# A norm's factors as a row through DRAM, and queries and keys of the retention computed transposed

## The chip, the cores and the metric

The kernel runs on one core of one Trainium2 chip. The metric is the device time of one execution in microseconds (us); lower is better. TensorE (PE in the profile) multiplies, VectorE (DVE) and ScalarE (ACT) work on its results, GpSimd (POOL) does little here, and SyncE (SP) issues nearly all DMAs, in one queue in order.

## The reference: what is computed

A trunk of two layers on x of 256 positions and 1024 columns, batch 1. Each layer has a half-step SwiGLU feed-forward (FFN, inner width 2816), a mixer, and another half-step FFN; each of these stands between a pre-norm and a post-norm and is added to x:

```python
h = swiglu(rms_norm(x, g[0]), ...);  x = x + 0.5 * rms_norm(h, g[1])
m = mixer(rms_norm(x, g[2]), ...);   x = x + rms_norm(m, g[3])
h = swiglu(rms_norm(x, g[4]), ...);  x = x + 0.5 * rms_norm(h, g[5])
```

`rms_norm(x, g)` is x times the position's factor 1/sqrt(mean(x^2) + eps), times the gain g of the column. Layer 0's mixer is dilated sliding-window attention (three groups of heads, their outputs merged); layer 1's is retention: 4 heads, one projection into queries q and keys k (256 columns a head each), values v (512) and two gates g_f and g_b (512 each), a rotation of q and k by the position's angles, and

```python
y_f = chunk_retention(q, k, v, log_gamma[0])              # decayed scores, forward
y_b = flip(chunk_retention(flip(q), flip(k), flip(v), log_gamma[1]))
y = silu(g_f) * head_group_norm(y_f) + silu(g_b) * head_group_norm(y_b)
out = y @ w_out
```

The rotation mixes the two halves of a head's 256 columns: (t1 cos - t2 sin, t1 sin + t2 cos).

## The kernel before, in words

All is float32, with each product made of three faster ones: an operand is split into a high part (a rounded copy, `fp32r`) and a low part (the rest), and `mm3` (lines 190 to 194) or the loop of `unit_t` adds high x high, high x low and low x high in PSUM. x is split in transposed form: `pre_half` transposes x of one tile of 128 positions (PE), copies the high part (ACT) and subtracts the low part (DVE) into `xh`, `xl`.

**The norm's factors are applied late.** The pre-norm's gain goes into the weights as they are split; the factor of the position (`rstd`, a column with one number per partition and tile, made by `pre_stats` and `rsqrt` on DVE while the next stage's first matmuls run) is applied to the projection's result. Where positions lie on partitions, `rstd` is the scale of the instruction that reads the result. Where they lie along the free axis, a row of 256 factors on every partition is needed. `rows` (lines 389 to 399) makes it: DVE multiplies the identity with each column of factors (`dg`), PE multiplies a matrix of ones with these diagonals (`rw`), DVE copies the result (`rows`). It is called once in each FFN and twice in attention (for q with the factor -0.125 in it, and for k).

**The weights' stream** (`Stream`). Weights come in loads of 1 MB (`dma`, line 83, or two loads of half a megabyte where a group takes columns from two places, as the retention's q and k) into two buffers `raw`. Each load makes two pieces; `split` makes a piece's high part on ACT and low part on DVE (lines 115 to 125) into a ring of six slots `w`, or, for the later pieces of a stage's first unit, into spare buffers (`wx`). When PE has used a piece, `done` splits the next one, and when a load's second piece is split the next load is issued. Pieces marked `still` lie at an offset of 16 elements in their slot.

**Units.** A projection goes in units of up to 512 columns, four pieces each, accumulated in two of six PSUM banks (`acc`). There are two forms. `unit` (lines 331 to 337) keeps x stationary and streams 512 columns of weights: 48 matmuls, results with positions on partitions ("natural"). `unit_t` (lines 368 to 387) keeps weights stationary and streams the 256 positions: 96 matmuls, results with columns on partitions ("transposed"). The first unit of each stage (`first_unit`) is natural, one tile of positions after the other, since x's second tile is ready later. In each unit, after the second piece, `flush` runs what was put into the list `pend`, and after every piece `work` runs two entries of the list `bg`. These lists and the order of the code give priorities; a scheduler orders each engine's instructions from them, ahead of the run, and the order on each engine is then fixed. DVE's order in the last part of a stage is that of the code.

**FFN** (`ffn`, `ffn_t`). Unit 0 (gate) and unit 1 (up) are natural, units 2 to 10 transposed; their gate results are multiplied with the row (line 350) before ACT's Silu. `rows` is put into `pend`, so that it runs in the middle of unit 1. Then comes `down`, the second projection.

**Attention** (`attn`). Units of q and k are transposed except the first; DVE multiplies them with the row while it stores them (line 662), q reversed within blocks of 64.

**Retention** (`plan_ret`, `ret`). For each head four natural units: q and k together ("qk"), v, g_f, g_b. At the start the rotation's tables (`rope`, positions on partitions) are scaled with `rstd` (line 872). After a qk unit DVE rotates each tile: two products with the tables (line 922), a difference and a sum (lines 925, 926) into `ro`. `rt_qk` (line 934) transposes the eight blocks of 128 x 128 on PE, and ACT copies them (line 935). `rt_scores` makes the scores of both chunks (line 944), multiplies them with the decay (line 946) and splits them; `rt_y` makes y forward (d = 0) or backward (d = 1); `rt_gate` normalises y and multiplies it with the Silu of the gate; `rt_store` transposes the sum and splits it for the output projection. In head 0 six empty entries stand ahead of the transposes and the scores in `bg`, so that they come at the end of the v unit and in the g_f unit; in heads 1 to 3 the transposes and the scores come after the second piece of the v unit.

The program's parts are, in this order: FFN, attention, FFN, FFN, retention, FFN. Every name of a tile in the profile leaves out numbers: `ac_f` are an FFN's accumulators, `at` attention's, `rt` the retention's, `d_f`, `d_at`, `d_rt` those of the second projections, `rqk` the transposed queries and keys, `rs` the scores, `rc` the tile that holds the copies of queries and keys and the decayed scores, `epsn` a reordered column of numbers that the second FFN moves by 4-byte DMAs, `gpost` the gain of a post-norm that is broadcast to all partitions.

## Time and profile before

| | |
|---|---|
| device time, median of 3 runs (lowest to highest) | 1292.06 us (1289.16 to 1293.95) |
| profiled execution: its device time | 1295.78 us |
| profiled execution: span from first to last instruction | 1294.0 us |
| mean granted TensorE clock | 0.998 |
| ScalarE and VectorE busy, of the span | 54% and 69% |
| first projection matmul of the retention to the last | 846.39 to 1054.1 us |

The device time of an execution is a little longer than the span of its instructions. Rows of a timeline give start, duration, engine, line, operation, tile written <- tiles read, shapes and the count of merged instructions; in brackets stands how long the engine idled before it and what ended that. Rows of the waits give who waited for whom, the total in us, the times, and the longest. Rows of one tile give minimum, median and maximum duration in ns. PE's matmuls are pipelined: a matmul's duration in a row is longer than the time from its start to the next one's start, so only the latter may be added up.

### The profile page before, as it was taken

The page shows a single profiled execution, that of the slowest core. Times are in us where ns is not written, and L with a number is a line of the kernel's source. Part 1 is how long each engine was busy: PE and PEld are TensorE (multiplying, and loading weights), DVE is VectorE, ACT ScalarE, POOL GpSimd, SP SyncE. Part 2 cuts the span into 40 slices and gives each one's busy share as a digit, 9 for nine tenths or more (in the row PEclk, how much of TensorE's full clock was granted, in tenths as well). Part 3 has the DMA queues.
Part 4 walks back from the last instruction along what each step waited for, and adds up shares of the span by engine and source line. Part 5 has one row for each costly group of instructions (what it writes and reads, how often), then busy time and mean ns, then how long its engine had stood idle before and what let it go on. Part 6 is the DMA issues. An engine that isn't in the chain of part 4 may idle for free.

```text
span 1294.0 us, 20715 instructions
## 1 busy us (share of the span) xinstructions
PE 1276.6 (99%) x8362; PEld 1136.7 (88%) x8362; DVE 889.4 (69%) x1593; ACT 695.5 (54%) x1073; POOL 19.7 (2%) x17
## 2 busy tenths in 40 slices
PE   8999999999999999999999999999999999999997
PEld 6999888987997879999889998877888888899986
DVE  6776557678567668866477665588887875767644
ACT  4655445467445557764456554455555545555442
POOL 1000001000000000000000000000000000000000
PEclk9999999999999999999999999999999999999999
DMA  7755566664764356665546565645564645565551
GB/s 217 229 186 193 189 217 192 200 200 146 201 198 153 130 162 221 196 196 179 192 163 209 187 195 194 197 147 175 155 184 144 186 165 195 168 200 176 190 195 65
DMA packets 130093, 235.72 MB, mean 182 GB/s; under 512 B 25404, under 2 KB 42284, under 8 KB 129997
## 3 DMA queue, kind: packets, MB, share of 16 engines
q1 hardware_dynamic: 129852, 234.14, 56.7%
q8 instruction: 65, 1.06, 0.3%
q14 instruction: 32, 0.25, 0.1%
q10 hardware_dynamic: 144, 0.26, 0.1%
HBM read 232.21 MB, written 1.12 MB: 180 GB/s over the span
## 4 chain that ended last, share of the span: by engine, by line
PE 90%; DVE 4%; ACT 2%; DMA 2%; issue 1%; SPq 0%; DVEq 0%; ACTq 0%
PE ac_f L381 10%; PE ac_f L382 10%; PE ac_f L383 10%; PE d_f L192 6%; PE d_f L193 6%; PE d_f L194 6%; PE rt L194 4%; PE rt L193 4%; PE rt L192 4%; PE at L382 3%; PE at L383 3%; PE at L381 3%; PE at L192 2%; PE at L194 2%; DMA raw<-in_ret_w_in_dram 2%; PE at L193 2%
## 5 line engine op out<-in xcount | busy, mean ns | idle before, releaser
L121 ACT ACTIVATE w<-raw,gcol 128x512 fp32r<-128x512 f32 x596 | 394.0, 715 | 309.0 <-PE ac_f L383 101.9
L122 DVE SCALAR_TENSOR_TENSOR w<-raw,gcol,w 128x512 fp32r<-128x512 f32 x596 | 418.1, 749 | 153.9 <-ACT w L121 150.6
L116 DVE TENSOR_TENSOR w<-raw,w 128x1024 fp32r<-128x1024 f32 x112 | 137.2, 1225 | 134.5 <-ACT w L115 134.2
L115 ACT ACTIVATE w<-raw 128x1024 fp32r<-128x1024 f32 x112 | 118.8, 1061 | 166.7 <-PE d_f L194 95.7
L192 PE MATMUL d_f<-w,hhf 128*128 128x512 f32 x352 | 137.2, 390 | 0.0
L193 PE MATMUL d_f<-w,hhf 128*128 128x512 f32 x352 | 137.0, 389 | 0.0
L194 PE MATMUL d_f<-w,hlf 128*128 128x512 f32 x352 | 137.0, 389 | 0.0
L382 PE MATMUL at<-xl_f,w 128*128 128x256 f32 x352 | 99.0, 281 | 0.0
L381 PE MATMUL at<-xh_f,w 128*128 128x256 f32 x352 | 99.0, 282 | 0.0
L383 PE MATMUL at<-xh_f,w 128*128 128x256 f32 x352 | 98.9, 281 | 0.0
L192 PE MATMUL rt<-w,xh_f 128*128 128x512 f32 x244 | 95.6, 392 | 0.2 <-ACT xh_f L238 0.2
L193 PE MATMUL rt<-w,xh_f 128*128 128x512 f32 x244 | 95.8, 392 | 0.0
L194 PE MATMUL rt<-w,xl_f 128*128 128x512 f32 x244 | 95.1, 390 | 0.0
L381 PE MATMUL ac_f<-xh_at,w 128*128 128x256 f32 x288 | 81.0, 281 | 0.0
L381 PE MATMUL ac_f<-xh_f,w 128*128 128x256 f32 x288 | 81.0, 281 | 0.0
L381 PE MATMUL ac_f<-xh_rt,w 128*128 128x256 f32 x288 | 81.0, 281 | 0.0
L383 PE MATMUL ac_f<-xh_f,w 128*128 128x256 f32 x288 | 80.9, 281 | 0.0
L383 PE MATMUL ac_f<-xh_rt,w 128*128 128x256 f32 x288 | 80.9, 281 | 0.0
L383 PE MATMUL ac_f<-xh_at,w 128*128 128x256 f32 x288 | 80.9, 281 | 0.0
L382 PE MATMUL ac_f<-xl_at,w 128*128 128x256 f32 x288 | 80.9, 281 | 0.0
L382 PE MATMUL ac_f<-xl_f,w 128*128 128x256 f32 x288 | 80.9, 281 | 0.0
L382 PE MATMUL ac_f<-xl_rt,w 128*128 128x256 f32 x288 | 80.9, 281 | 0.0
(346 smaller groups left out, 2835.8 us busy)
## 6 DMA issues: line engine op xcount, KB each, us to landing
raw<-in_ffn_w_down_dram SPq DMA_DIRECT2D x44, 1024.0 KB, 4.9
raw<-in_ffn_w_up_dram SPq DMA_DIRECT2D x40, 1024.0 KB, 5.0
raw<-in_ffn_w_gate_dram SPq DMA_DIRECT2D x39, 1024.0 KB, 5.0
raw<-in_attn_w_in_dram SPq DMA_DIRECT2D x36, 1024.0 KB, 5.1
raw<-in_ret_w_in_dram SPq DMA_DIRECT2D x24, 1024.0 KB, 5.6
raw<-in_ret_w_in_dram SPq DMA_DIRECT2D x16, 512.0 KB, 3.9
raw<-in_ret_w_out_dram SPq DMA_DIRECT2D x8, 1024.0 KB, 4.8
raw<-in_ffn_w_gate_dram SPq DMA_DIRECT2D x10, 512.0 KB, 4.0
```

Of the source, the lines that this page charges most:

```text
L115: nc.scalar.activation(hi, raw, AF.Copy)
L116: nc.vector.tensor_tensor(out=lo, in0=raw, in1=hi.bitcast(F32), op=ALU.subtract)
L121: nc.scalar.activation(hi[:, s], raw[:, s], AF.Copy, scale=gc)
L122: nc.vector.scalar_tensor_tensor(out=lo[:, s], in0=raw[:, s], scalar=gc, in1=hi[:, s].bitcast(F32), op0=ALU.mult, op1=ALU.subtract,)
L192: mm(out, xh, wh, start=start, stop=False)
L193: mm(out, xh, wl, start=False, stop=False)
L194: mm(out, xl, wh, start=False, stop=stop)
L381: mm(out, hi[:, s], xh, start=k == 0 and a == 0, stop=False, skip_group_check=True)
L382: mm(out, hi[:, s], xl, start=False, stop=False, skip_group_check=True)
L383: mm(out, lo[:, s], xh, start=False, stop=k == NK - 1, skip_group_check=True)
```

## The change

Three things, in one edit:

- `rows` and the matrix of ones go. `row_out` stores `rstd`, two numbers per partition, as 256 numbers in a row in DRAM (one DMA on SP), right behind the first unit of each FFN, of attention and of retention. `row_in` loads this row into every partition (one DMA on SP); it stands in `pend`, so in the middle of the second unit. FFNs take this row where they took `rows`; attention takes it for q and k, with the factor -0.125 now in the instruction, which for that becomes two half as wide.
- In retention the qk units are transposed ones (`unit_t`, pieces `still`), so that queries and keys come out of PSUM with the head's columns on partitions. The rotation's tables come transposed from the host's constants, cos and sin of all 256 positions beside each other; they are multiplied once with the row (in the second unit). The rotation makes, for q and for k, two products and a difference and a sum, and writes into the place from which the scores are made. The 32 transposes and 8 ACT copies of `rt_qk` go.
- In head 0 the units' order is g_f, qk, v, g_b instead of qk, v, g_f, g_b, so that the first unit remains natural. The Silu of g_f is made after the first unit; y forward, its gate and y backward are put into `bg` together, after the v unit. The six empty entries go.

The core of the diff:

```diff
-        self.ones = sb.tile([P, P], F32, name="ones")
-        nc.gpsimd.memset(self.ones, 1.0)
...
-            r = st["r"].unsqueeze(1).to_broadcast([P, 2, 2 * P])
+            r = self.row.unsqueeze(1).to_broadcast([P, 2, 2 * P])
...
-    def rows(self, cols, name):
...
+    def row_out(self, name):
+        self.factors = self.dram.tile([2 * P], F32, name=f"factors_{name}")
+        self.nc.sync.dma_start(self.factors[0 : 2 * P].rearrange("(t p) -> p t", p=P), self.rstd)
+
+    def row_in(self, name):
+        self.row = self.sb.tile([P, 2 * P], F32, tag="row", name=f"row_{name}")
+        self.nc.sync.dma_start(self.row, self.factors[0 : 2 * P].partition_broadcast(P))
...
                 self.first_unit(pieces, accs)
-                self.pend.append(lambda: st.update(r=self.rows(self.rstd, "f")))
+                self.row_out(name)
+                self.pend.append(lambda: self.row_in(name))
...
-                self.pend.append(lambda rq=rq: scales.update(q=self.rows(rq, "q"), k=self.rows(self.rstd, "k")))
+                self.row_out("at")
+                self.pend.append(lambda: self.row_in("at"))
...
-                        nc.vector.tensor_tensor(out=dst, in0=src, in1=sc.unsqueeze(1).to_broadcast([P, 2, 4, 64]), op=ALU.mult)
+                        for a in range(2):
+                            nc.vector.scalar_tensor_tensor(out=dst[:, a], in0=src[:, a], scalar=-0.125 if kind == "q" else 1.0, in1=sc, op0=ALU.mult, op1=ALU.mult)
...
-            units.append((h, "qk", self.ws.add_rows([w[:, q : q + 256], w[:, D + q : D + q + 256]], NK, n)))
...
+            for kind in ("qk", "v", "gf", "gb") if h else ("gf", "qk", "v", "gb"):
+                if kind == "qk":
+                    units.append((h, kind, self.ws.add_rows([w[:, q : q + 256], w[:, D + q : D + q + 256]], NK, n, True)))
...
                 self.first_unit(pieces, accs)
-                for t in range(2):
-                    nc.vector.tensor_scalar(out=self.rope[t], in0=self.rope[t], scalar1=self.rstd[:, t : t + 1], scalar2=None, op0=ALU.mult)
+                self.row_out("rt")
+                self.pend.append(lambda: self.row_in("rt"))
             else:
-                self.unit(pieces, accs)
+                (self.unit_t if kind == "qk" else self.unit)(pieces, accs)
             if kind == "qk":
+                if u == 1:
+                    nc.vector.tensor_tensor(out=self.rope, in0=self.rope, in1=self.row.unsqueeze(1).to_broadcast([P, 2, 2 * P]), op=ALU.mult)
...
-                if h:
-                    self.pend.append(lambda st=st: self.rt_qk(st))
-                    self.pend.append(lambda st=st: self.bg.append(lambda: self.rt_scores(st)))
-                else:
-                    skip = lambda: None
-                    self.bg += [skip] * 6 + [lambda st=st: self.rt_qk(st, (0,)), lambda st=st: self.rt_qk(st, (1,)), lambda st=st: self.rt_scores(st), skip]
+                for b in range(2):
+                    self.rotary(st, b, accs[b])
+                self.pend.append(lambda st=st: self.bg.append(lambda: self.rt_scores(st)))
...
                 self.bg.append(lambda st=st: self.rt_y(st, 0))
+                if h == 0:
+                    self.bg += [lambda st=st, sg=sg: self.rt_gate(st, 0, sg), lambda st=st: self.rt_y(st, 1)]
...
-                if d == 0:
+                if u == 0:
+                    pass
+                elif d == 0:
...
+        for i in range(2):
+            z = sb.tile([P, 512], F32, tag="pr", bufs=6, name=f"m{i}{st['h']}{b}")
+            m.append(z.rearrange("p (a c) -> p a c", a=2))
+            nc.vector.tensor_tensor(out=m[i], in0=a, in1=self.rope[:, ::-1] if i else self.rope, op=ALU.mult)
+        nc.vector.tensor_tensor(out=st["qk"][:, 2 * b, :], in0=m[0][:, 0], in1=m[0][:, 1], op=ALU.subtract)
+        nc.vector.tensor_tensor(out=st["qk"][:, 2 * b + 1, :], in0=m[1][:, 0], in1=m[1][:, 1], op=ALU.add)
```

More of the change, by code (lines that the diff above doesn't have):

```diff
@@ L387, in unit_t @@
             self.work(quota)
-    def rows(self, cols, name):
-        nc, sb = self.nc, self.sb
-        d = sb.tile([P, 2, P], F32, tag="dg", name=f"dg_{name}")
-        for t in range(2):
-            nc.vector.tensor_scalar(out=d[:, t, :], in0=self.ident, scalar1=cols[:, t : t + 1], scalar2=None, op0=ALU.mult)
-        tr = self.trb(f"rw_{name}")
-        nc.tensor.matmul(tr[:, : 2 * P], self.ones, d, start=True, stop=True)
-        r = sb.tile([P, 2 * P], F32, tag="rowsq" if name == "f" else f"rows{name}", name=f"rows{name}")
-        nc.vector.tensor_copy(r, tr[:, : 2 * P])
-        return r
+    def row_out(self, name):
[4 more added lines that the diff above has]
+        self.nc.sync.dma_start(self.row, self.factors[0 : 2 * P].partition_broadcast(P))
     def flush(self):
@@ L620, in attn @@
         rq = ru = None
-        scales = {}
-        tasks_o1 = None
         for u, (o, kind, g, pieces) in enumerate(plan["units"]):
@@ L658, in attn @@
                         src = accs[b].rearrange("p (a r i) -> p a r i", a=2, r=4)
-                        sc = scales[kind].rearrange("p (r i) -> p r i", r=4)
+                        sc = self.row.rearrange("p (r i) -> p r i", r=4)
                         if kind == "q":
                             src, sc = src[:, :, :, ::-1], sc[:, :, ::-1]
-                        nc.vector.tensor_tensor(out=dst, in0=src, in1=sc.unsqueeze(1).to_broadcast([P, 2, 4, 64]), op=ALU.mult)
+                        for a in range(2):
+                            nc.vector.scalar_tensor_tensor(out=dst[:, a], in0=src[:, a], scalar=-0.125 if kind == "q" else 1.0, in1=sc, op0=ALU.mult, op1=ALU.mult)
                 for t in range(2 if u == 0 else 0):
@@ L810, in plan_ret @@
             q, v = h * 256, 2048 + h * 512
-            units.append((h, "qk", self.ws.add_rows([w[:, q : q + 256], w[:, D + q : D + q + 256]], NK, n)))
-            for i, kind in enumerate(("v", "gf", "gb")):
-                c = v + i * 2048
-                units.append((h, kind, self.ws.add_rows([w[:, c : c + 512]], NK, n)))
+            for kind in ("qk", "v", "gf", "gb") if h else ("gf", "qk", "v", "gb"):
+                if kind == "qk":
+                    units.append((h, kind, self.ws.add_rows([w[:, q : q + 256], w[:, D + q : D + q + 256]], NK, n, True)))
+                else:
+                    c = v + ("v", "gf", "gb").index(kind) * 2048
+                    units.append((h, kind, self.ws.add_rows([w[:, c : c + 512]], NK, n)))
         return dict(units=units, out=self.ws.add_down(self.ret_w_out[j], 16), l=l, j=j)
@@ L855, in ret_tables @@
                 nc.vector.tensor_tensor(out=self.dec[:, dd, h, :], in0=self.dec[:, dd, h, :], in1=msk[:, dd, :], op=ALU.mult)
-        self.rope = [tab[:, 2048 + 256 * t : 2304 + 256 * t].rearrange("p (a c) -> p a c", a=2) for t in range(2)]
-        for t in range(2):
-            nc.sync.dma_start(tab[:, 2048 + 256 * t : 2304 + 256 * t], self.c_rope[t * P : (t + 1) * P, :])
+        self.rope = tab[:, 2048:2560].rearrange("p (a c) -> p a c", a=2)
+        nc.sync.dma_start(tab[:, 2048:2560], self.c_rope)
     def ret(self, plan, nxt):
@@ L913, in ret, with rotary @@
         self.down(plan["out"], 16, hT, {3: self.flush}, gb, "rt", nxt)
-    def rotary(self, st, t, acc):
+    def rotary(self, st, b, acc):
         nc, sb = self.nc, self.sb
-        h = st["h"]
-        a = acc.rearrange("p (b c) -> p b c", c=P)
-        m1 = sb.tile([P, 512], F32, tag="pr", bufs=6, name=f"m1{h}{t}")
-        m2 = sb.tile([P, 512], F32, tag="pr", bufs=6, name=f"m2{h}{t}")
-        for m, i in ((m1, 0), (m2, 1)):
-            nc.vector.tensor_tensor(out=m.rearrange("p (b c) -> p b c", c=P), in0=a, in1=self.rope[t][:, i : i + 1, :].to_broadcast([P, 4, P]), op=ALU.mult)
-        ro = sb.tile([P, 512], F32, tag="h", bufs=2, name=f"ro{h}{t}")
-        v1, v2, vo = (z.rearrange("p (b s c) -> p b s c", b=2, s=2) for z in (m1, m2, ro))
-        nc.vector.tensor_tensor(out=vo[:, :, 0, :], in0=v1[:, :, 0, :], in1=v2[:, :, 1, :], op=ALU.subtract)
-        nc.vector.tensor_tensor(out=vo[:, :, 1, :], in0=v2[:, :, 0, :], in1=v1[:, :, 1, :], op=ALU.add)
-        st["ro", t] = ro
-    def rt_qk(self, st, tiles=(0, 1)):
-        nc = self.nc
-        for t in tiles:
-            tr = self.trb(f"rqk{st['h']}{t}")
-            for b in range(4):
-                nc.tensor.transpose(tr[:, b * P : (b + 1) * P], st["ro", t][:, b * P : (b + 1) * P], self.ident)
-            nc.scalar.activation(st["qk"][:, :, t * P : (t + 1) * P], tr.rearrange("p (b c) -> p b c", c=P), AF.Copy)
+        a = acc.rearrange("p (a c) -> p a c", a=2)
+        m = []
+        for i in range(2):
[4 more added lines that the diff above has]
+        nc.vector.tensor_tensor(out=st["qk"][:, 2 * b + 1, :], in0=m[1][:, 0], in1=m[1][:, 1], op=ALU.add)
     def rt_scores(self, st):
@@ L1031, in constants @@
     ang = np.arange(256, dtype=np.float32)[:, None] * inv.astype(np.float32)[None, :]
-    rope = np.concatenate([np.cos(ang), np.sin(ang)], axis=1).astype(np.float32)
+    rope = np.concatenate([np.cos(ang).T, np.sin(ang).T], axis=1).astype(np.float32)
     return {"c_onehot": oh.reshape(33, 9 * 128), "c_rope": rope}
```

3 lines of the change are left out of this document (removed).

## The prediction

> **What bounds the kernel now.** I read the page first: its first line, the busy times and the line of the chain that ended last.
>
> ```profile
> span 1294.0 us, 20715 instructions
> PE 1276.6 (99%) x8362; PEld 1136.7 (88%) x8362; DVE 889.4 (69%) x1593; ACT 695.5 (54%) x1073; POOL 19.7 (2%) x17
> PE 90%; DVE 4%; ACT 2%; DMA 2%; issue 1%; SPq 0%; DVEq 0%; ACTq 0%
> ```
>
> TensorE (PE) carries 90% of the chain. The other engines matter only where PE stands still for them, so I then read the waits of PE alone. Three of their rows touch the change:
>
> ```profile
> PE rw_f L396 <- DVE dg_f L394: 1.8, 1, 1.8
> PE ac_f L192 <- ACT w L121: 1.3, 1, 1.3
> PE rs L944 <- ACT rc L935: 0.9, 1, 0.9
> ```
>
> In 1294 us PE waits for weights once, for 1.3 us. It waits once for the diagonal of the norm's factors and once for the copies of the transposed queries and keys; both of these waits go with the change. So the price of an edit is the PE time it takes out or puts in, as long as the weights stay ahead. PE's time is read from the starts of successive matmuls; their durations overlap.
>
> **The two forms of a projection.** The units of queries and keys go from moving weights (48 matmuls of 512 columns) to stationary weights (96 of 256). Both forms stand in the FFNs. In PE's timeline, 38 matmuls of the first form stand between and including the first pair of rows, 79 of the second form between and including the second pair:
>
> ```profile
> 480.69 0.39 PE L193 MATMUL ac_f<-wx,xh_at 128*128 128x512 f32 x1
> ...
> 489.08 0.39 PE L193 MATMUL ac_f<-w,xh_at 128*128 128x512 f32 x1
> ```
>
> ```profile
> 502.10 0.28 PE L382 MATMUL ac_f<-xl_at,w 128*128 128x256 f32 x1
> ...
> 511.28 0.28 PE L382 MATMUL ac_f<-xl_at,w 128*128 128x256 f32 x1
> ```
>
> That is 8.39/37 = 0.2268 us and 9.18/78 = 0.1177 us from start to start. A unit takes 48 x 0.2268 = 10.89 us or 96 x 0.1177 = 11.30 us, so each of the four units gets 0.41 us longer: **+1.7 us**, all on PE. The Trainium skill ("TensorE: Matmul & The Clock Gate", Back-to-back issue gap) gives a warm matmul N/2.4 + 2.5 ns; by it the units would differ by an estimated 96 x 109.2 - 48 x 215.8 ns = 0.12 us, 0.5 us for four. The measured pitch carries some 11 to 13 ns beyond the columns, not 2.5, and halving the columns doubles how often it is paid.
>
> **The transposes that go.** Each head loses eight transposes (L934) and two ScalarE copies (L935). For head 1:
>
> ```profile
> 917.30 0.40 PE L194 MATMUL rt<-w,xl_f 128*128 128x512 f32 x1
> 917.53 1.04 PE L934 MATMUL rqk<-ident,ro 128*128 128x128 f32 x8
> ...
> 919.79 0.40 PE L192 MATMUL rt<-w,xh_f 128*128 128x512 f32 x1
> ```
>
> From 917.30 to 919.79 are 2.49 us; seven projection matmuls start in it, 7 x 0.2268 = 1.59. The eight transposes cost 0.90 us, four heads **-3.6 us**. The eight copies took ScalarE about 0.6 us each, off the path.
>
> **The row that goes through DRAM.** Four FFNs lose one `rows` (two DVE products with the identity, a matmul with ones, a DVE copy), attention loses two, so six matmul groups go. The start of the second FFN and of the first:
>
> ```profile
> 489.30 0.39 PE L194 MATMUL ac_f<-w,xl_at 128*128 128x512 f32 x1
> 489.53 0.59 PE L396 MATMUL rw_f<-dg_f,ones 128*128 128x256 f32 x2
> ...
> 492.28 0.39 PE L193 MATMUL ac_f<-w,xh_at 128*128 128x512 f32 x1
> ```
>
> ```profile
> 30.11 0.39 PE L193 MATMUL ac_f<-w,xh_in 128*128 128x512 f32 x1
> 32.26 0.67 PE L396 MATMUL rw_f<-dg_f,ones 128*128 128x256 f32 x2 [1.76 <-DVE dg_f L394]
> 33.01 0.40 PE L192 MATMUL ac_f<-w,xh_in 128*128 128x512 f32 x1
> 33.76 2.74 DVE L122 SCALAR_TENSOR_TENSOR w<-raw,gcol,w 128x512 fp32r<-128x512 f32 x4 [0.37 <-ACT w L121]
> 37.80 0.28 PE L381 MATMUL ac_f<-xh_in,w 128*128 128x256 f32 x1
> ```
>
> In the second FFN 2.98 us hold eleven matmuls, 2.49 us; the group costs 0.49. In the first, 33.01 - 30.11 = 2.90 hold two, so it costs 2.45 with its wait. What is late next there? PE would reach the first transposed unit at 37.80 - 2.45 = 35.35 instead. Half of the four splits from 33.76 make its first piece, ready at about 35.1: it just fits, so I count the whole. Five times 0.49 and 2.45: **-4.9 us**. If that weight comes later by as much as PE comes earlier, at most 2.2 of it is lost.
>
> What is added in place of the group is a store of 256 four-byte elements and a load of 128 rows of 1 KB on SP, the queue of all weights. No row shows a store of this shape, or any wait for its landing. Nearest are the four-byte moves of eps, which wait for the very computation that ends in rstd, and the load of the post-norm gain, also broadcast to all partitions. Their issues and landings (minimum, median, maximum; eps, then gain):
>
> ```profile
> 482.49 0.37 SPq L83 DMA_DIRECT2D raw<-in_ffn_w_gate_dram  x1
> 484.98 1.74 SPq L437 DMA_DIRECT2D epsn<-eps_pre_at  x3
> 487.67 0.37 SPq L83 DMA_DIRECT2D raw<-in_ffn_w_gate_dram  x1
> DMA to landing us min/median/max: 2.5/3.9/4.7
> DMA to landing us min/median/max: 3.8/4.3/4.9
> ```
>
> I take 3.9 for the store and 4.3 for the load: the row stands about 0.6 + 3.9 + 0.5 + 4.3 = 9.3 us after rstd, with 0.6 and 0.5 for the two issues. An FFN first uses it at the end of its third unit, over 20 us later. Attention and retention use it at the end of their second unit. Their rstd, and attention's first use (the first two rows are attention, the last retention):
>
> ```profile
> 214.30 0.17 DVE L221 TENSOR_SCALAR rstd_f<-nw_pre_f 128x2 f32<-128x2 f32 x1
> 227.31 1.40 DVE L662 TENSOR_TENSOR qk<-at,rowsk 128x512 f32<-128x512 f32 x2 [2.25 <-PE at L383]
> 860.10 0.17 DVE L221 TENSOR_SCALAR rstd_f<-nw_pre_f 128x2 f32<-128x2 f32 x1
> ```
>
> 214.5 + 9.3 = 223.8 is before 227.3. In retention 860.3 + 9.3 = 869.6; the second unit, beginning at about 859.5, ends at 859.5 + 11.3 = 870.8. So the row costs nothing on PE, by 3.5 us and by 1.2 us. With both moves at their longest and a weight load of 5 us in front, it would be late; that is a rival below.
>
> The store waits at the head of SP, and the load waits for the store; behind both stand the loads of weights. What does that delay? In the third FFN (SP, DVE, DVE, PE):
>
> ```profile
> 670.05 5.53 SPq L83 DMA_DIRECT2D raw<-in_ffn_w_gate_dram  x2
> 672.27 0.17 DVE L221 TENSOR_SCALAR rstd_f<-nw_pre_f 128x2 f32<-128x2 f32 x1
> 675.96 2.74 DVE L122 SCALAR_TENSOR_TENSOR w<-raw,gcol,w 128x512 fp32r<-128x512 f32 x4 [0.42 <-ACT w L121]
> 683.00 0.28 PE L381 MATMUL ac_f<-xh_f,w 128*128 128x256 f32 x1
> ```
>
> The load issued at 670.05 becomes two pieces from 675.96 on, the first ready at 677.3 and used at 683.0: 5.7 us in hand. rstd comes at 672.4, when SP idles before the second of the two loads (670.05 + 5.53 less an issue of 0.37: 675.2). Store and load fit about that gap; a second load late by 2 to 3 us stays inside what is in hand. I take nothing, with the bounds 0 and the rival's price.
>
> **VectorE and the order.** In attention 22 products of 512 columns become 44 of 256, and the wider ones of the scores' product are the nearest row of that kind:
>
> ```profile
> L946 DVE SCALAR_TENSOR_TENSOR rc<-rs,rtab x16: 281/348/425, 878.2 to 1025.5; 128x256 f32<-128x256 f32 x8, 128x128 f32<-128x128 f32 x8
> 876.19 1.99 PE L944 MATMUL rs<-rc 128*128 128x256 f32 x8 [0.94 <-ACT rc L935]
> ```
>
> At 0.425 twice instead of 0.70 (the row at 227.31, 1.40 for two) a pair costs 0.15 us more, 3.3 us spread over 22 places, where VectorE sits 2.25 us idle before the use at 227.3: nothing on PE. The rotation keeps its operations and widths; one product with the row replaces two scalings. In head 0 the 0.94 us wait of the scores (last row) loses its cause, the copies; what can be late next is the row, the scaling of the tables and the rotation. Gate, values and scores of head 0 also come closer together: first outputs, their gate and second outputs all fall into one unit. I count half of the wait, **-0.5**; the bounds are -0.9 and +2 (the same wait doubled).
>
> **The sum:** +1.7 - 3.6 - 4.9 - 0.5 = -7.3 us. The profiled execution took 1295.78 us for its span of 1294.0, 3.7 above the median of the three times; it would come to 1288.5, the median to 1292.06 - 7.3 = **1284.8**. About 0.5% (6.5 us) is what a measurement can tell from no change; the forecast lies only just beyond it.
>
> **The rivals.** *The row is late in attention and retention.* Both moves at their longest and a weight load ahead: 0.6 + 4.7 + 5.0 + 0.5 + 4.9 = 15.7 us after rstd, that is 230.2 in attention (2.9 late, which the weights in hand cover) and 876.0 in retention, 5.2 late. Rotation and scores of head 0 follow, and PE's order is fixed, so PE waits about 5 us: 1284.8 + 5.2 = 1290. For it speaks the margin of 1.2 us in retention; against it that loads rarely stand in front, SP idling before most of them.
>
> *The queue is held: slower.* If the store is put ahead of the load of 670.05, that load waits for rstd (2.4 us), then, with the row's load right behind the store, for the store's landing L, with 0.8 us for issues: L + 3.2 us late against 5.7 in hand. Per stage PE loses L - 2.5, six stages 6L - 15. At L = 4.7 that is 13 us, 6 more than the gain; at 6.6, the landing of attention's loads of short rows below, 24.6, so 1284.8 + 24.6 = 1309.
>
> ```profile
> bias<-lines SPq DMA_DIRECT2D x8, 512.0 KB, 6.6
> ```
>
> It decides for slower than 0.5% from L = 4.8. Against it stands where the moves of eps were put: after the load of 482.49, not before it. The Trainium skill ("DMA: Bandwidth & Descriptors", Specifications) says that transfers of under 512 B are carried out as read-modify-write; that speaks for a long L with 4-byte elements in DRAM, and no row here shows it.
>
> *The stationary form costs retention nothing*, both forms streaming 24,576 columns: then +1.7 becomes about 0, 1283.1. Against it: the pitch of 0.1177 us held over 79 matmuls.
>
> **How the numbers follow.** The forecast has 0.70, the late row 0.17, the held queue 0.07, the free form 0.06. Within the forecast the unknowns (-0.4 to +2.5 in head 0, up to +2.2 at the start, some 1.5 of the median's own spread, as the three times differ by 4.8) put about 0.3 of it at less than 6.5 us of gain. Faster: 0.70 x 0.7 + 0.06 = 0.55; same: 0.21 + 0.17 = 0.38; slower 0.07. The range reaches from 1281.5, the free form with the whole wait gone and 1 us of spread, to 1290.5, which holds the late row.
>
> **What would show it.** The lines of L934 and L396 gone from PE; the query and key units at 0.1177 us a matmul; no wait of PE at the start of the first FFN; the span of the retention's projections shorter by 3.6 + 0.5 - 1.7 = 2.4 us; row loads landing within 10 us of rstd; no new PE wait for `w`. Wrong would be: PE waits for weights behind the row's moves, a DVE wait for the row with PE waiting for it, or a stationary unit in retention far from 11.3 us.

## The result, and the profile after

| | before | after |
|---|---|---|
| time, median of the runs (us) | 1292.64 (4 runs, 1289.16 to 1293.95) | 1313.06 (4 runs, 1309.07 to 1319.96) |
| ratio, 95% interval | | 1.016 [1.0126, 1.0195] |
| the profiled execution (us) | 1295.78 | 1310.38 |
| its span (us) | 1294.0 | 1308.6 |

The change is slower by 20.4 us in the medians. The forecast was 1284.8, faster; the range ended at 1290.5. The page of the changed kernel, its first line, the busy times and the sums of the chain (the work that ended last, followed back from the last instruction to what released each step):

```profile
span 1308.6 us, 21008 instructions
PE 1269.2 (97%) x8510; PEld 1136.4 (87%) x8510; DVE 879.2 (67%) x1596; ACT 690.8 (53%) x1064; POOL 19.2 (1%) x16
PE 81%; DVE 8%; DMA 7%; ACT 2%; issue 1%; SPq 0%; DVEq 0%; ACTq 0%
```

PE is busy 7.4 us less than before (1276.6); how much of that is the edit's can't be read here, since the rhythm of its matmuls and its granted clock (0.989 after, 0.998 before), both below, move it too. Yet the span is 14.6 us longer: PE is idle for 39.4 us of it and was idle for 17.4. It carries 81% of the chain where it carried 90%; DMA and DVE took its place. So PE waits. The waits of PE in the changed kernel, largest first (total us, times, longest):

```profile
PE htr L411 <- DVE h_f L471: 9.6, 3, 3.9
PE rs L932 <- DVE rc L922: 6.6, 1, 6.6
PE ac_f L379 <- ACT w L121: 5.7, 1, 5.7
PE ac_f L190 <- ACT w L121: 2.0, 1, 2.0
```

None of them stood in the profile before at more than 1.3 us. The first is the transposes of the hidden values in three FFNs, the second head 0 of the retention, the third the first transposed unit of the first FFN: these lie in the stretch after a stage's rstd. The fourth is the wait for the kernel's first weight, over at 10.0 us, ahead of any store; the kernel before has it too, and it took 1.3 to 3.9 us in the traces of this case. What do the engines that release PE wait for? In the waits of ACT, the loads of the FFNs' gate weights, before and then after:

```profile
ACT w L121 <- DMA raw<-in_ffn_w_gate_dram: 20.0, 15, 2.7
```

```profile
ACT w L121 <- DMA raw<-in_ffn_w_gate_dram: 59.7, 22, 10.2
```

ACT, which makes the high part of each weight, waited 2.7 us at most for a weight and now waits up to 10.2 us. The third FFN shows where that comes from. SP's issues, then ACT, in the changed kernel:

```profile
674.60 0.37 SPq L83 DMA_DIRECT2D raw<-in_ffn_w_gate_dram  x1
677.01 0.37 SPq L390 DMA_DIRECT2D factors_f<-rstd_f  x1
679.76 0.37 SPq L83 DMA_DIRECT2D raw<-in_ffn_w_gate_dram  x1
686.63 0.34 SPq L394 DMA_DIRECT2D row_f<-factors_f  x1
688.31 0.37 SPq L83 DMA_DIRECT2D raw<-in_ffn_w_up_dram  x1
```

```profile
684.79 2.56 ACT L121 ACTIVATE w<-raw,gcol 128x512 fp32r<-128x512 f32 x4 [6.44 <-DMA raw<-in_ffn_w_gate_dram]
691.55 2.56 ACT L121 ACTIVATE w<-raw,gcol 128x512 fp32r<-128x512 f32 x4 [4.20 <-DMA raw<-in_ffn_w_gate_dram]
```

The store is issued at 677.01, and the row's load, which waits for it, at 686.63: 9.6 us. The two weight loads to either side of the store, issued at 674.60 and 679.76, were not held back by any wait on SP, and their data still reach ACT only at 684.8 and 691.5. The chain of waits gives the second of them 11.70 us, and its like in the first and second FFN no less:

```profile
29.12 12.52 DMA raw<-in_ffn_w_gate_dram
...
493.03 11.80 DMA raw<-in_ffn_w_gate_dram
679.76 11.70 DMA raw<-in_ffn_w_gate_dram
```

The prediction's working had 5 us for such a load. What the DMA engines do meanwhile, from the windows of each kernel, before and after. A row gives the window, its length, the busy us (and instructions) of PE, PEld, DVE, ACT and POOL, the granted clock, the busy share of the DMA engines and GB/s:

```profile
676.00:684.00 8.00, 8.00 (x41) 6.77 (x40) 5.97 (x10) 4.33 (x7) 0.00 (x0) 1.00 0.81 264
```

```profile
680.00:688.00 8.00, 8.00 (x40) 6.75 (x40) 2.46 (x4) 2.56 (x4) 0.00 (x0) 1.00 0.67 44
```

For 8 us the engines are 67% busy and move a sixth of the bytes. So the queue doesn't stand idle behind a wait; packets are in flight and are slow to end. The trace's records of single packets show it: the 4-byte writes are over by 679.5, 0.6 us after the first of them, though the store lands at 686.6; the 2 KB packets of the weights take 0.08 us in the median, but up to 6.1 us in this stretch, where none of the same stretch before takes more than 0.9. Behind the other five stores, windows of 8 us show 31, 52, 32, 94 and 31 GB/s (attention 52, the retention 94). The landings of the changed kernel's moves (name, KB, median us):

```profile
epsn<-eps_pre_at SPq DMA_DIRECT2D x8, 0.1 KB, 10.0
...
factors_at<-rstd_f SPq DMA_DIRECT2D x1, 1.0 KB, 9.8
factors_f<-rstd_at SPq DMA_DIRECT2D x1, 1.0 KB, 9.3
```

The five stores whose landing is known land in 9.1 to 9.8 us, and the moves of eps beside them, 3.9 before, in 10.0.

**What the change was to bring to the retention is there.** Head 1 and head 2, from start to start, before and after:

```profile
900.31:951.65 51.34, 51.34 (x235) 42.52 (x234) 42.40 (x91) 27.83 (x44) 0.00 (x0) 1.00 0.54 165
951.65:1003.00 51.35, 51.35 (x236) 42.52 (x235) 42.41 (x91) 27.85 (x44) 0.00 (x0) 1.00 0.55 164
```

```profile
851.45:915.10 63.65, 54.67 (x275) 45.57 (x274) 45.73 (x113) 26.53 (x44) 2.77 (x1) 0.92 0.53 143
915.10:965.77 50.67, 50.67 (x275) 44.11 (x274) 43.00 (x97) 27.02 (x42) 0.00 (x0) 1.00 0.51 152
965.77:1016.45 50.68, 50.68 (x276) 44.12 (x274) 42.52 (x91) 27.01 (x42) 0.00 (x0) 1.00 0.55 166
```

Heads 1 and 2 are 0.67 us shorter each. Head 0 (first row of the second fence) takes 63.65 us; before it ran from 846.39 to 900.31, 53.92. It has a store in it.

**One correction before stages are compared.** The starts of the stationary matmuls (256 columns) stand either 113.3 or 117.8 ns apart, for most of a stage, and which of the two holds differs from stage to stage and from run to run (last section). An FFN has some 850 of them, so the rhythm alone moves it by up to 3.8 us. The table adds 4.5 ns for each start that the trace shows at 113.3 ns, and so sets all stages to the slow rhythm, as if PE set the pace everywhere (an estimate); the runs of the next section stand beside. Stages run from the first transpose of x to the next stage's; the first FFN so holds the wait for the kernel's first weight. Lengths in us:

| stage | before | after | store alone | row on PE | wide row | wide row, old retention |
|---|---|---|---|---|---|---|
| FFN 1 | 195.9 | 203.2 | 201.4 | 197.1 | 196.9 | 196.2 |
| attention | 270.3 | 269.9 | 271.1 | 270.5 | 270.4 | 270.4 |
| FFN 2 | 187.7 | 190.6 | 189.7 | 187.7 | 187.7 | 187.6 |
| FFN 3 | 187.6 | 191.6 | 193.3 | 187.5 | 187.6 | 187.5 |
| retention | 253.2 | 261.0 | 261.6 | 250.9 | 250.1 | 253.8 |
| FFN 4 | 196.6 | 202.0 | 199.6 | 196.5 | 196.8 | 196.9 |

In the profiled executions the changed kernel had the fast rhythm in FFN 2 to 4 (800 to 813 fast starts each) where the kernel before had the slow one. It lost 27.0 us by this table, of which 12.1 came back by the rhythm and 0.3 by an earlier first transpose; 14.6 are left in the spans. The medians, 20.4, lie between. The store alone, which had the fast rhythm in the same three stages, lost 25.4 by the table.

### The profile page after: what moved, and what is told of

It is laid out like the page before. It is cut to its first block, busy times and chain, and to the rows that moved or that the text cites. A ratio compares the mean times of both kernels' runs of the same rounds, so it can differ in the third digit from the quotient of the medians.

```text
span 1308.6 us, 21008 instructions
## 1 busy us (share of the span) xinstructions
PE 1269.2 (97%) x8510; PEld 1136.4 (87%) x8510; DVE 879.2 (67%) x1596; ACT 690.8 (53%) x1064; POOL 19.2 (1%) x16
## 3 DMA queue, kind: packets, MB, share of 16 engines
q8 instruction: 66, 1.08, 0.3%
## 4 chain that ended last, share of the span: by engine, by line
PE 81%; DVE 8%; DMA 7%; ACT 2%; issue 1%; SPq 0%; DVEq 0%; ACTq 0%
PE ac_f L379 10%; PE ac_f L381 10%; PE ac_f L380 10%; PE d_f L192 6%; PE d_f L190 6%; PE d_f L191 6%; DMA raw<-in_ffn_w_gate_dram 5%; DVE w L122 3%; PE at L380 3%; PE at L379 3%; PE at L381 3%; PE rt L190 3%; PE rt L191 3%; PE rt L192 3%; PE at L190 1%; PE at L192 1%
## 5 line engine op out<-in xcount | busy, mean ns | idle before, releaser
L379 PE MATMUL ac_f<-xh_in,w 128*128 128x256 f32 x288 | 81.3, 282 | 5.7 <-ACT w L121 5.7
L381 PE MATMUL ac_f<-xh_in,w 128*128 128x256 f32 x288 | 80.9, 281 | 0.0
L380 PE MATMUL ac_f<-xl_in,w 128*128 128x256 f32 x288 | 80.6, 280 | 0.0
```

The source lines that it names most:

```text
L379: mm(out, hi[:, s], xh, start=k == 0 and a == 0, stop=False, skip_group_check=True)
L380: mm(out, hi[:, s], xl, start=False, stop=False, skip_group_check=True)
L381: mm(out, lo[:, s], xh, start=False, stop=k == NK - 1, skip_group_check=True)
```

## The experiments

Theory 1: the store itself holds up the DMA engines, whoever waits for it. Its rivals: the order of head 0 costs the time (2), or SP, held until the store lands (3). The kernels of one batch ran beside runs of the kernel before, whose median was 1293.41 in the first two batches of four; ratios are taken within a batch.

### The row on TensorE again, in the changed kernel

```diff
-        self.nc.sync.dma_start(self.factors[0 : 2 * P].rearrange("(t p) -> p t", p=P), self.rstd)
...
-        self.nc.sync.dma_start(self.row, self.factors[0 : 2 * P].partition_broadcast(P))
+        d = sb.tile([P, 2, P], F32, tag="dg", name=f"dg_{name}")
+        for t in range(2):
+            nc.vector.tensor_scalar(out=d[:, t, :], in0=self.ident, scalar1=self.rstd[:, t : t + 1], scalar2=None, op0=ALU.mult)
+        tr = self.trb(f"rw_{name}")
+        nc.tensor.matmul(tr[:, : 2 * P], self.ones, d, start=True, stop=True)
...
+        nc.vector.tensor_copy(self.row, tr[:, : 2 * P])
```

> The changed kernel with one part undone: the row of factors comes from the matmul with ones again (one call per stage, retention included), nothing goes through DRAM. Theory 1, the scattered 4-byte store holds up the DMA rings, and the late row and late weights are all of the loss: the waits of 6.6 us (scores of head 0) and 5.7 us (first FFN) are gone, heads 1 to 3 stay at 50.7 us each, and the time is 1 to 3 us under the kernel before (three heads at -0.67, one matmul group saved in attention, one added in retention), so about 1290. Theory 2, the new order of head 0 makes the scores late by itself: a wait of about 6 us stays before the scores of head 0, and the time is 4 to 8 us over the kernel before.

Measured: 1290.18 us, ratio 0.9971 [0.9953, 0.9989]. No long stall is left in head 0 (PE waits 1.1 us for its scores); the retention takes 250.9 us against 253.2. This is what theory 1 expected. So the order of head 0 and the transposed form aren't what costs; theory 2 falls.

### The store alone, in the kernel before

```diff
+    def probe(self):
+        self.probes = getattr(self, "probes", 0) + 1
+        f = self.dram.tile([2 * P], F32, name=f"probe{self.probes}")
+        self.nc.sync.dma_start(f[0 : 2 * P].rearrange("(t p) -> p t", p=P), self.rstd)
```

It is called at the six places where the change stores; nobody reads what it writes.

> The kernel before with one thing added: the store of the 256 factors of 4 bytes at the same six places. Nobody reads it and nothing waits for it. Theory 1, the store holds up the DMA rings by itself: it lands 9 to 10 us after its issue as in the changed kernel, the load of weights behind it takes 10 to 12 us instead of 5, and the time rises by 5 to 12 us, most of it at the start and at the start of retention. Theory 3, the loss comes from SP standing in front of the row's load until the store has landed, with weights queued behind: here SP never waits for the store, loads of weights keep their 5 us, and the time stays within 2 us of the kernel before.

Measured: 1310.94 us, ratio 1.0129 [1.0104, 1.0153]: 17.5 us by the medians, more than the 5 to 12 expected. The waits of PE and the landings:

```profile
PE htr L421 <- DVE h_f L481: 7.2, 3, 2.8
PE rqk L942 <- DVE ro L933: 6.7, 1, 6.7
PE ac_f L381 <- ACT w L121: 3.3, 1, 3.3
```

```profile
probe<-rstd_f SPq DMA_DIRECT2D x3, 1.0 KB, 10.3
probe<-rstd_in SPq DMA_DIRECT2D x1, 1.0 KB, 9.0
```

These are the changed kernel's waits, at the same three places, in a kernel that has neither the row's load nor any wait for the store. Theory 1 is shown, and theory 3 falls as the cause of the loss: here SP waits for no store to land.

### The same store, its elements 512 bytes apart

```diff
-        f = self.dram.tile([2 * P], F32, name=f"probe{self.probes}")
-        self.nc.sync.dma_start(f[0 : 2 * P].rearrange("(t p) -> p t", p=P), self.rstd)
+        f = self.dram.tile([2 * P * P], F32, name=f"probe{self.probes}")
+        self.nc.sync.dma_start(f[0 : 2 * P * P].rearrange("(t p c) -> p t c", p=P, c=P)[:, :, 0:1], self.rstd.unsqueeze(2))
```

> As the run with the store alone, but each of the 256 elements of 4 bytes goes to a place of its own in DRAM, 512 bytes from the next. Theory 1a, the writes get in each other's way because all fall into the same 1 KB: the store lands in under 5 us, weights behind it keep about 5 us, and the time is that of the kernel before within 2 us. Theory 1b, a 4-byte write to DRAM is slow wherever it goes: landing 9 to 10 us and the same loss as with the packed store.

Measured: 1294.23 us, ratio 0.9999 [0.9982, 1.0016]. The landings:

```profile
probe<-rstd_f SPq DMA_DIRECT2D x3, 1.0 KB, 3.1
probe<-rstd_in SPq DMA_DIRECT2D x1, 1.0 KB, 1.5
```

As many elements of 4 bytes, from the same queue at the same places, cost nothing that can be measured when they don't fall into one kilobyte: they land in 1.5 to 3.1 us against 8.5 to 10.3, so the size of an element alone doesn't decide. The Trainium skill ("DMA: Bandwidth & Descriptors", Specifications) has transfers of under 512 B carried out as read-modify-write. Taken by itself as a rule of cost, that would make the spread store as slow as the packed one, which it is not.

### Half the writes, and elements 64 bytes apart

Two more forms of the store in the kernel before. The first writes each partition's two factors as one element of 8 bytes into the same kilobyte:

```diff
-        self.nc.sync.dma_start(f[0 : 2 * P].rearrange("(t p) -> p t", p=P), self.rstd)
+        self.nc.sync.dma_start(f[0 : 2 * P].rearrange("(p t) -> p t", t=2), self.rstd)
```

> The kernel before plus the six stores, nobody waiting for them, now as 128 elements of 8 bytes (each partition's two factors side by side) into the same 1 KB, in place of 256 of 4 bytes. If the time goes with the number of writes that fall into one place, half the writes give about half the delay: the stores land in 5 to 6 us, and the whole takes about 1302 us (ratio about 1.006). If it goes with the place alone, or with the bytes, nothing changes from the 256 writes: landings of 8.5 to 10 us, about 1310 us (1.013).

Measured: 1298.15 us, ratio 1.0044 [1.0021, 1.0066], less than the 1302 expected of half the writes. One long wait of PE is left, in head 0 of the retention:

```profile
PE rqk L942 <- DVE ro L933: 4.7, 1, 4.7
```

The second:

```diff
-        f = self.dram.tile([2 * P], F32, name=f"probe{self.probes}")
+        f = self.dram.tile([2 * P * 16], F32, name=f"probe{self.probes}")
...
+        self.nc.sync.dma_start(f[0 : 2 * P * 16].rearrange("(t p c) -> p t c", p=P, c=16)[:, :, 0:1], self.rstd.unsqueeze(2))
```

> The kernel before plus the six stores of 256 elements of 4 bytes, nobody waiting for them, each element now 64 bytes from the next (16 KB in all). If what collides are writes to the same 64 bytes or less, they land as the ones spread by 512 bytes did, in 1.5 to 3.1 us, and the time is that of before, about 1294 us (ratio 1.000). If what collides is larger, 512 bytes say, eight writes still share each place: landings between 3 and 9 us and a time between 1296 and 1310 us.

Measured: 1295.58 us, ratio 1.0011 [0.9987, 1.0035]. The landings, of the pairs and of the pitch of 64 bytes:

```profile
probe<-rstd_f SPq DMA_DIRECT2D x3, 1.0 KB, 6.3
probe<-rstd_in SPq DMA_DIRECT2D x1, 1.0 KB, 4.4
```

```profile
probe<-rstd_f SPq DMA_DIRECT2D x3, 1.0 KB, 3.5
probe<-rstd_in SPq DMA_DIRECT2D x1, 1.0 KB, 1.5
```

The delay goes with the number of writes into one place, at equal bytes: 128 writes fewer land 4.0 and 4.6 us sooner in these two rows, 31 to 36 ns for each (the other two stores, 2.8 and 3.2 us, 22 to 25 ns). The time falls faster than the landing (5 us lost against 17): in the FFNs the shorter delay fits into the weights that are in hand, and mainly the retention is longer than before (258.3 us against 253.2). With 64 bytes between the elements nothing is lost that can be measured. How close writes must lie to collide is not shown by that: eight writes in 512 bytes would cost 0.3 us by the same 31 to 36 ns (an estimate), if several places are served at once, and that is too little to see here.

### The row's load set free

The changed kernel with its stores, but the row is loaded from 256 gains instead of from what was stored; this kernel so applies gains in place of factors.

```diff
-        self.nc.sync.dma_start(self.row, self.factors[0 : 2 * P].partition_broadcast(P))
+        self.nc.sync.dma_start(self.row, self.norm_gains[0, 0, 0 : 2 * P].partition_broadcast(P))
```

> The changed kernel with its stores as they are, but the row is loaded from 256 gains of an input and not from what was stored, so this kernel applies gains in place of the norm's factors there. The load then waits for nothing, SP is not held for the store's landing, and the row is never late. If all of the loss is the rings standing still behind the store, the time stays that of the changed kernel, about 1313 us (ratio 1.016). If the held queue and the late row come on top of it, they go: the store alone costs about 16.7 us and the rest of the change brings 7.3, so about 1302 us (1.007). If the hold alone were the loss, about 1285 us (0.994).

Measured: 1309.83 us, ratio 1.0109 [1.0077, 1.0142], against 1.016 [1.0126, 1.0195] of the changed kernel. It lies between the first two answers, nearer to the first. It is 3.2 us less than the changed kernel by the medians, 0.5% by the ratios, whose intervals overlap, and 0.8 us by the spans of the two traces. So the held queue and the late row may add a few us to what the store costs, and perhaps nothing; the loss stays without them. Head 0 shows why so little. VectorE in the changed kernel, then with the free load:

```profile
882.19 0.69 DVE L874 TENSOR_TENSOR rtab<-rtab,row_rt 128x512 f32<-128x512 f32 x1 [10.35 <-DMA row_rt<-factors_rt]
```

```profile
882.28 2.74 DVE L122 SCALAR_TENSOR_TENSOR w<-raw,gcol,w 128x512 fp32r<-128x512 f32 x4 [5.77 <-ACT w L121]
```

In the first, DVE waits 10.35 us for the row, until 882.19. In the second DVE doesn't wait for the row at all, and it goes on at 882.28, when the weight arrives that was held up too; in the changed kernel ACT gets that weight at 881.92. Two waits end together; to take one away brings nothing, and a reader of the first row alone would have named the wrong one.

### The row as two elements of 512 bytes

The changed kernel with rstd transposed on PE to two partitions, copied, and stored from there.

```diff
-        self.nc.sync.dma_start(self.factors[0 : 2 * P].rearrange("(t p) -> p t", p=P), self.rstd)
+        tr = self.trb(f"rt2_{name}")
+        self.nc.tensor.transpose(tr[:2, :P], self.rstd, self.ident)
+        w = self.sb.tile([2, P], F32, tag="wide", name=f"wide_{name}")
+        self.nc.vector.tensor_copy(w, tr[:2, :P])
+        self.nc.sync.dma_start(self.factors[0 : 2 * P].rearrange("(t p) -> t p", p=P), w)
```

> The changed kernel with the store made wide: TensorE transposes the two columns of factors into two partitions, VectorE copies them, and the store writes two rows of 512 bytes; the load into all partitions is unchanged. Theory 1: the store lands in 2 to 4 us, the load within 5, no wait of PE for weights behind them, the wait of the scores of head 0 under 1.5 us, and the time falls 3 to 8 us under the kernel before, to about 1287. Theory 2, the order of head 0: the 6 us wait of the scores stays, 1290 to 1296. Theory 3, SP held by the row's load: the hold shrinks with the landing, part of the loss stays where weights are short, 1288 to 1293.

Measured: 1284.89 us, ratio 0.9931 [0.991, 0.9952]: faster than both. The largest of its waits of PE, which is the one for the kernel's first weight, and the one ahead of the first transpose of rstd:

```profile
PE ac_f L190 <- ACT w L121: 2.5, 1, 2.5
...
PE rt_f L391 <- DVE eps_pre_in L223: 1.0, 1, 1.0
```

Neither weights nor scores are waited for behind the store. SP still carries the row's load behind the store, but it is held for less: in the third FFN the row's load goes 4.5 us behind the store, with SP standing still for at most 1.2 us of them. So this run by itself doesn't tell the hold from the landing; the store alone and the free load do. How much of the gain is the row's? The same row in the kernel before, its retention untouched (in attention likewise):

```diff
-                self.pend.append(lambda: st.update(r=self.rows(self.rstd, "f")))
+                self.row_out(name)
+                self.pend.append(lambda: self.row_in(name))
```

> The kernel before with its retention untouched but for the row, and the row sent through DRAM from two partitions as two elements of 512 bytes (as in the version that was faster than both). If the prediction's terms were right in themselves, the row's part is about -4.9 us less what the transposes of the factors cost, and the retention's part -2.4: this kernel takes 1286 to 1289 us (ratio 0.995 to 0.997), between before and the version with both. If the gain of that version came all from the retention's order and form, this one equals before (0.999 to 1.001).

Measured: 1291.44 us, ratio 0.9978 [0.9956, 1.0], between the two answers. By the table its stages equal those of before within 0.6 us each, so the row through DRAM saves no work that can be seen, and what is saved lies in the retention (250.1 against 253.2).

### Both good versions again

The work of the wide row and of the row on PE differs by 0.7 us in the table, and their medians by 5.3. Both once more, side by side, with new runs of the kernel before beside them (1295.94):

> The version with the row from two partitions and the changed retention a second time, on another chip, with five rounds. If what it gained is in its work, the ratio is again 0.991 to 0.995. Its profiled execution, with the two rhythms of the stationary matmuls set equal in both traces, is only 2 us shorter than that of before, nearly all of it in the retention (250.1 against 253.2 us); if the rest was the rhythm's luck, the ratio is 0.996 to 0.999.

> The changed kernel with its rows made on TensorE, one a stage, a second time beside the one above. Its retention is as short (250.9 us against 253.2), so by the work alone the two are within 1 us of each other, at a ratio of 0.996 to 0.999 each. If the row through DRAM in two elements is worth more than the matmul with ones, this one is slower than the other by 3 us or more, as it was (1290.2 against 1284.9).

Measured: 1288.14 us, ratio 0.9939 [0.9921, 0.9958], and 1292.25 us, ratio 0.9982 [0.9967, 0.9998]. The difference comes back, 4.1 us, against the expectation that the two would be within 1 us, and the wide row's ratio lies in the range that was to mean that its gain is work. The sums of the stages with rhythms set equal don't show it: 1289.5 and 1289.3 for the wide row against 1290.2 and 1288.4, and 1291.3 before. What differs in the traces is the rhythm: both profiles of the wide row ran FFN 3 at 113.3 ns (813 starts each), both of the row on PE at 117.8, though one of these ran FFN 4 fast (813), and that execution was the shortest of its twelve. So the wide row is faster than the kernel before by 0.6 to 0.7%, and by the table some 2 us of that are work that went away. That the rest is how often a stage gets the fast rhythm is argued from four profiles; the other executions have no trace, and it stays open.

## Why the prediction was wrong, point by point

**The step that failed** stands in the paragraph on the row: "I take 3.9 for the store", from the moves of eps, and behind it "I take nothing, with the bounds 0 and the rival's price". The eps moves were near in element size alone: each moves 32 elements into SBUF, into as many partitions, where the store puts 256 into one kilobyte of DRAM. The store took 9.1 to 9.8 us. But even 9.8 in the prediction's own scheme would have been read wrongly, since the scheme has only one way for a store to cost: someone waits for it. What it left out is that the store slows the other transfers: a weight load beside it took 11.7 us instead of 5, at 44 GB/s instead of 264. In the store-alone kernel nobody waits for the store, and it lost 17.5 us, the whole change 20.4.

**The rival that had the sign**, the held queue, gave 1309 for L = 6.6 by 6L - 15; for the measured L of 9.6 it gives 42.6 us of loss and 1327. So its 1309, near the 1313 measured, is luck. Its mechanism was not it: in the third FFN the store stood between the two gate loads, where the prediction put it, and SP wasn't held for the next load: it went 5.16 us after the one before (674.60, 679.76), as before the change (670.05 and 5.16 later). The loads were slow on their way. The load behind the row's was issued 1.3 us after the row's, so it too waited for something else by then. In the retention the load behind the row's went 7.3 us after the one before; with the free load, where SP waits for no store to land, it went 8.1 us after. The chance of 7 in 100 was too little for a term with no row behind it.

**The late row** (1290): the row was late, first used in head 0 at 882.19, 17.2 us after rstd (865.03) where 9.3 were worked out, but weights were late to the same moment.

**+1.7, the stationary form**: right. Head 1's unit of queries and keys runs from 915.10 to 927.29 after, 12.19 us with what lies between, and from 900.31 to 912.09 before, 11.78: 0.41 more, as predicted. **-3.6, the transposes**: the rest of head 1 went from 39.56 to 38.48 us, -1.08 a head against -0.90: right, a fifth too small. **-0.5, head 0**: without a store in the way head 0 takes 53.35 us with the row on PE, 0.57 less than before, where the three terms made 0.99; that version has a group with ones in its retention, 0.49 by the prediction's own price, which the kernel before hasn't. With the wide row it takes 52.42, 1.50 less. Together -2.4 was predicted for the retention; -2.3 to -3.1 came in the versions without the packed store.

**-4.9, the groups of the row**: not there in any run as a gain. With the wide row, FFN 2 and FFN 3 take 187.7 and 187.6 us, as with the old groups; the transpose of rstd took the place of the group at about its price (0.4 us by the starts around it, against 0.49). With the packed store no transpose is needed, but PE then stands before weights that are held up, so that PE time saved ahead of the weights is waited for behind them: the store alone lost 17.5 us, and the whole change, predicted 7.3 better than that, lost 20.4. In attention alone the changed kernel is 1.2 us shorter than the store alone, where two groups were to bring 1.0. No run shows the groups gone with nothing in their place. The 2.45 at the start has, in the changed kernel, the answer that the prediction weighed: "if that weight comes later". PE reached the first transposed unit early and waited there for its weight:

```profile
42.50 0.58 PE L379 MATMUL ac_f<-xh_in,w 128*128 128x256 f32 x1 [5.65 <-ACT w L121]
```

The load of 29.12 with its 12.52 us is the cause of the 5.65. With the wide row this wait is gone; its first FFN, less the wait for the kernel's first weight, takes 194.4 us against 194.6 before. There the transpose waits 1.0 us for rstd, in place of the group's 1.8.

**VectorE's halved products**: attention is within 0.4 us of before in the versions without the packed store and in the changed kernel. The wide row's versions wait 1.1 to 1.3 us there for VectorE once (`pr`, in the softmax), which the kernel before doesn't; whether the halved products cause it, no run shows.

**What was to show it** held in part: the pitch of 117.7 ns in the units of queries and keys, the lines of L934 and L396 gone; "PE waits for weights behind the row's moves" was the stated sign of being wrong, and it is what the profile shows.

**The number met by another kernel**: the wide row's first median, 1284.89, is the 1284.8 that was forecast. That is luck: by the table its work is 2 us less than before, not 7.3, and its second median was 1288.14, beside 1295.94 for the kernel before.

## What to carry to other kernels

A store of one small element per partition, packed into one short stretch of DRAM, is a load on every transfer in flight, and not only on its reader: here each of six stores of 256 writes of 4 bytes into 1 KB cut the transfers to 31 to 94 GB/s for some 8 us. Gather such values onto few partitions first, or, where the reader allows it, write them 64 bytes apart (no run here reads a row from there). And where a trace has no row for a shape, ask which property of the nearest row made it cheap, and give the other case a chance to match.

## What the runs showed of the hardware

**Writes to one place hold up the loads around them.** 256 writes of 4 bytes into 1 KB land in 8.5 to 10.3 us; the same at 64 or 512 bytes apart in 1.5 to 3.5. Meanwhile the loads of weights, the one issued 2.4 us ahead of the store too, run at 44 GB/s instead of 264 (third FFN), with the DMA engines 67% busy. Whether the writes wait for each other in the memory or on the way to it, no run here shows.

**A stall can cost PE more than its length.** The windows behind the wait of the first FFN (5.7 us, until 42.50) and around that of the third (2.8 us, until 695.70) in the changed kernel (the granted clock is the third number from the end):

```profile
40.20:47.00 6.80, 4.50 (x19) 4.22 (x20) 4.52 (x7) 5.13 (x8) 0.00 (x0) 0.50 0.69 236
691.00:695.50 4.50, 1.90 (x17) 1.69 (x15) 3.19 (x5) 3.09 (x5) 0.00 (x0) 1.00 0.68 239
695.50:699.00 3.50, 3.30 (x16) 3.30 (x17) 3.39 (x6) 2.03 (x4) 0.00 (x0) 0.51 0.77 256
699.00:705.00 6.00, 6.00 (x55) 6.00 (x55) 4.01 (x7) 4.56 (x8) 0.00 (x0) 1.00 0.71 210
```

After 2.8 us without a matmul the granted clock is 0.51 for 3.5 us: another 1.7 us lost. It is 0.50 behind the waits of head 0 (6.6 us) and of the last FFN (3.9 us) too. PE so works for some 16 us at half clock behind these four waits; that is about 8 us by estimate, if nothing else held PE there. Not each wait brings it: behind the 2.9 us in the second FFN the clock stays at 1.00, and behind 2.0 us in the third FFN of the free load it is 0.50 for 3.4 us. The Trainium skill ("TensorE: Matmul & The Clock Gate", What's actually happening) has the clock at half after an idle window of about 3.4 us and full again after as long a busy one; the recovery of 3.5 us agrees, and the 2.8 us of PE's idle, and the 2.0 more so, are less than the window that it names.

**Stationary matmuls have two rhythms.** To see whether a stage sets its rhythm, the kernel before got one transpose of the identity ahead of each unit with stationary weights:

```diff
+        tr = self.trb(f"probe{self.probes}")
+        self.nc.tensor.transpose(tr[:, :P], self.ident, self.ident)
```

> On what the traces showed beside the question: a stage's matmuls with stationary weights start either every 113.3 ns or every 117.8 ns, for as long as the stage lasts, and a few of the changes stand at an interruption. This is the kernel before with one transpose of the identity, which nobody reads, ahead of each unit with stationary weights. If any interruption draws the rhythm anew, both rhythms stand mixed within each FFN, in which 6 to 11 units then begin with one. If the stage (its operands, where they lie) sets it, the second, third and fourth FFN keep 117.8 ns as in the profile before. The transposes themselves cost about 0.1 us each, some 6 us.

Measured: 1299.99 us in one run, 4.05 above the median of before on its chip. In its second FFN, the matmuls around one of these transposes:

```profile
505.70 0.28 PE L386 MATMUL ac_f<-xh_at,w 128*128 128x256 f32 x1
...
510.80 0.28 PE L386 MATMUL ac_f<-xh_at,w 128*128 128x256 f32 x1
510.92 0.27 PE L373 MATMUL probe<-ident 128*128 128x128 f32 x1
...
511.27 0.28 PE L386 MATMUL ac_f<-xh_at,w 128*128 128x256 f32 x1
...
522.22 0.28 PE L386 MATMUL ac_f<-xh_at,w 128*128 128x256 f32 x1
```

From 505.70 to 510.80 are 45 starts, 113.3 ns each; from 511.27 to 522.22 are 93, 117.7 ns each. Both rhythms stand mixed in each FFN, in the same order in FFN 2, 3 and 4, with 225 or 226 fast starts in each where the kernel before had none. In the changed kernel FFN 2, 3 and 4 begin with some 50 slow starts and turn fast behind the transposes that PE waited for, and so they do with the store alone. So the stage as a whole doesn't set it: an interruption can change it, not each one does, and no trace here shows a change without one. What decides at an interruption stays open. It moves a stage by up to 3.8 us, as much as most terms of the prediction, and it was no part of it: the 117.7 ns that the prediction read from one stage was one of two values.
